# Rows transposed inside a projection's last group, three tiles begun on each half, and decode held and repaid there

## The chip, the cores and the metric

The kernel runs on one core of one Trainium2 chip. The metric is the device time of one execution in microseconds (us); the time of a kernel is the median of its runs. The core has a matrix engine (TensorE, PE in the profile, with its weight loads shown as PEld), a vector engine (VectorE, DVE), a scalar engine (ScalarE, ACT), a general engine (GpSimd, POOL), which here also issues the gathers of the decode part, and SyncE (SP), whose queue issues most weight loads. Each engine works through its own instructions in the order in which they were written into its queue, and waits where an instruction's data or buffer is not ready.

## The reference

One step of a decoder layer on two groups that share the weights: a prompt of 1024 rows of width 1024, and 8 sample rows, each with 8192 cached positions. For the prompt, `x` passes three blocks, each added to it:

```
xp = xp + merge_heads(fox_prompt(q, k, v, logf), sgu_prompt(u, z, ...), ..., w_o)   # attention + gating, out-projection w_o
xp = xp + cross_attend(rmsnorm(xp, g_cross), mk, mv, w_cq, w_co)                    # 256 memory tokens, 4 heads
xp = xp + conv_ffn(rmsnorm(xp, g_ffn), 0, w_up, conv_w, conv_b, w_down)             # MLP with a width-3 convolution
y  = rmsnorm(xp, g_final)
```

The sample rows go through the same layer, with attention over the cached keys and values (`cache_k`, `cache_v`, found through a page table). All matrices are fp32, and the prompt's products are made to nearly fp32 accuracy.

## The kernel before, in words

**Products.** A prompt product of fp32 operands is made of three matmuls of a faster type: each operand is split into a high part (ACT copies it, L235 or L238) and a low part (DVE subtracts, L236 or L239), and high x high, high x low and low x high are added up in one PSUM bank (`gemm3`, L272 to L274; in `out_proj` the same three stand at L1055 to L1057 and L1073 to L1075). With 8 slices of the contracted width a tile of 128 x 512 takes 24 matmuls. PSUM banks come from two pools: `BA` (tag `ba`, four banks) and `BB` (tag `bb`, two); `MM`, `TR` and `BK` are one function that takes from them in turn.

**Order of the prompt.** The 1024 rows are done in two halves of 512 rows (four row tiles of 128), one after the other: output projection `out_proj` with `w_o` (the stage is called `mid`), cross attention `cross` with its own `out_proj` with `w_co`, then the MLP `ffn`. Between an `out_proj` and the product after it stand the row norm and a transposition, because the next product needs the rows' columns on the partitions. That happens four times: into `cross` and into `ffn`, for each half. I call these places seams.

**At a seam.** `out_proj` makes its second 512 columns in the groups of row tiles (0), (1) and (2, 3). After each group `residual` (L1007, DVE) adds the result to the rows, and ACT sums their squares (L230). In front of `ffn` the rows are also scaled by their norm (`factor` on ACT and POOL, L1023 and L1024; `scaled` and `both` on ACT, L1036 and L1037); in front of `cross` they are not, since the norm is applied to the scores later. Then `norm_T` takes tiles 0 and 1: per pair of slices four transposes (L1106) into one bank and two splits out of it, each on ACT and DVE; then it calls `first`, which makes one tile of the next product on the first 256 rows. Then the same for tiles 2 and 3, and the other 256 rows of that one tile. All other tiles of the next product are made on 512 rows at once.

**Decode beside the prompt.** The sample rows are a second stream. `decode` makes 128 steps: each gathers a chunk of keys (L1407, POOL), multiplies it by the query on DVE (L1423) and reduces it there (L1427); value chunks are gathered at L1469 and multiplied on TensorE (L1475). `sample_rest` does the rest of the layer for the sample rows. The prompt's code yields its expected time `t` at many places; the loop at the end adds `t` to `acc[0]` and runs one step of the second stream for each `PACE` of it. While `held[0]` is set no step is taken, but the time still adds up, and is paid afterwards, at most one step or so at a yield. `held[0]` is set after group (2, 3) and cleared at the end of `norm_T`. What stands in each engine's queue in the end, and where, is decided by a planner that puts the instructions in order.

Of the kernel before, what the change touches and what calls it, by code (L numbers as in the profile page):

```python
# [30 lines left out]
NF = FF // P  # L31
# [47 lines left out]
def build(nc, tc, ctx, a, phases=None):  # L79
# [935 lines left out]
    def out_proj(w, mh, ml, xt, fetch=None, ys=None):  # L1015
# [26 lines left out]
        for n in range(2):  # L1042
# [24 lines left out]
            for group in ((0,), (1,), (2, 3)):  # L1067
                pss = [MM() for _ in group]
                for k in korder:
                    wh, wl = (ws[k // 2][q][:, k % 2, :] for q in range(2))  # L1070
                    for i, ps in zip(group, pss):
                        tb = slice(i * P, (i + 1) * P)
                        mmul(ps, mh[k][:, tb], wh, start=(k == korder[0]), stop=False)  # L1073
                        mmul(ps, mh[k][:, tb], wl, start=False, stop=False)
                        mmul(ps, ml[k][:, tb], wh, start=False, stop=(k == korder[-1]))  # L1075
# [14 lines left out]
    def norm_T(ys, g0, first):  # L1090


        hs, ls = [], []
        for t0 in (0, 2):
# [3 lines left out]
            for kk in range(0, 8, 2):  # L1098
                if t0 == 0:
                    h2, l2 = U([P, 2, 512], F32R), U([P, 2, 512], F32R)  # L1100
                    hs += [h2[:, 0, :], h2[:, 1, :]]
                    ls += [l2[:, 0, :], l2[:, 1, :]]
                tr = TR()
# [16 lines left out]
    def cross(xt, sq):  # L1120
# [12 lines left out]
        ws = [wload(wpair(a["w_cq"], kk, 0, 512), 1024) for kk in range(4)]  # L1133
        q2, ps0 = [], MM()
# [8 lines left out]
        hs, ls = yield from norm_T(xt, G_CROSS, lambda hs, ls, c: products(ps0[:, c], ws, 0, hs, ls, c))  # L1143
# [61 lines left out]
        for n in range(2):  # L1205
            if n:
                ws = [wload(wpair(a["w_cq"], kk, n * 512, 512), 1024) for kk in range(4)]
            for dt_ in range(4):
                if dt_ % 2 == 0:
                    q2.append(U([P, 2, 512]))  # L1210
                if n or dt_:
                    ps = MM()
                    products(ps, ws, dt_, hs, ls, slice(0, 512))
                else:
                    ps = ps0
# [29 lines left out]
        sq = yield from out_proj(a["w_co"], oh, ol, xt, ys=ys)  # L1245
        return ys
# [4 lines left out]
    def ffn(hf, xt, ys, late=None):  # L1251
        w0, pv0 = wload(a["w_up"][0], 1024), BK()

# [4 lines left out]
        hs, ls = yield from norm_T(ys, G_FFN, lambda hs, ls, c: up(pv0[:, c], w0, hs, ls, c))  # L1258
# [11 lines left out]
        for gi, gn in enumerate(GROUPS):  # L1270
            gh, gl = [], []
            for f in range(f0, f0 + gn):
                hc2 = []
                for part in range(2):
# [3 lines left out]
                    if ft:  # L1278
                        w_, pv = wload(a["w_up"][ft], 1024), BK()
                        up(pv, w_, hs, ls, slice(0, 512))  # L1280
                    else:
                        pv = pv0
# [548 lines left out]
    def prompt():  # L1831
# [38 lines left out]
        for hf in range(2):  # L1870
# [10 lines left out]
            sq = yield from out_proj(a["w_o"], mh, ml, xt, partial(load_x, hf))  # L1881
            if hf == 0:
                ys = yield from mix(cross(xt, sq), gating(1), 0.05)
            else:
                ys = yield from cross(xt, sq)
            phase[0] = f"ffn{hf}"
            sq = yield from ffn(hf, xt, ys, (lambda: ahead.append(merge(*merge_in(1))) or ahead[0]) if hf == 0 else None)
# [11 lines left out]
    seen = 0  # L1899
    for t in prompt():  # L1900
# [8 lines left out]
        acc[0] += t  # L1909
# [102 lines left out]
```

## Time and profile before

| | us |
|---|---|
| median of 3 runs | 1816.22 (1815.31 to 1817.39) |
| the profiled execution | 1820.56, its span 1818.4 |
| TensorE busy | 1745.0 (96%) |
| VectorE busy | 1397.5 (77%) |
| ScalarE busy | 734.4 (40%) |
| mean granted TensorE clock | 0.986 |

How to read it: the profile shows one execution. A row of a group names the line, the engine, the operation, the tile written and the tiles read, the count, the busy time and the mean of one, and then the idle time in front of it with what ended it. "PE bb L273 <- DVE u L239" says that TensorE's instruction of L273 waited for DVE's of L239. In a row of a stretch stand its start and end, its length, the busy time of the five engines with the count of instructions, the granted clock, the share of the DMA engines and GB/s. TensorE's matmuls overlap in the records, so the time of one is read from the distance of two starts. The first half's seams lie near 547 us (into `cross`) and 707 us (into `ffn`), the second half's near 1183 and 1351 us; the MLPs lie behind 722 and behind 1365 us.

### The profile page before, as it was taken

The numbers are of one execution on the slowest core, as the hardware profiler recorded it, in microseconds if no ns is written. First come the engines' busy times: TensorE is split into PE (matmuls) and PEld (weight loads), VectorE is DVE, ScalarE is ACT, GpSimd is POOL, SyncE is SP. The second block draws the span as 40 slices with busy tenths as digits, with TensorE's granted clock in tenths as the row PEclk, the third lists the DMA queues.
The fourth block names the chain that finished last, engine by engine and source line by source line (L and its number), as shares of the span: only waits on it lengthen the run. The fifth ranks groups of instructions, "written<-read, shape, count | busy, mean of one in ns | idle before, by whom it ended". The sixth has DMA issues, their size and how long they took to land.

```text
span 1818.4 us, 25090 instructions
## 1 busy us (share of the span) xinstructions
PE 1745.0 (96%) x9637; PEld 1294.9 (71%) x9637; DVE 1397.5 (77%) x1729; ACT 734.4 (40%) x1378; POOL 510.0 (28%) x461
## 2 busy tenths in 40 slices
PE   8999999888998999999999999989899999999997
PEld 5887776656676767777777776766576778767775
DVE  4689668888788877999989899898875549845344
ACT  6332365455643544433333244235353324332332
POOL 1252334332133432223332333334222111011110
PEclk9999999899999999999999999989999999999999
DMA  8886889777696986679878779988787777568982
GB/s 295 306 297 231 302 297 329 242 266 224 219 398 257 342 310 260 257 285 340 316 279 311 271 306 340 381 300 324 290 309 290 267 268 265 179 266 289 359 314 82
DMA packets 157074, 521.06 MB, mean 287 GB/s; under 512 B 20874, under 2 KB 40842, under 8 KB 124186
## 3 DMA queue, kind: packets, MB, share of 16 engines
q0 software_dynamic: 57168, 341.14, 49.5%
q1 hardware_dynamic: 92874, 165.73, 26.4%
q10 hardware_dynamic: 6912, 12.59, 1.8%
q8 instruction: 76, 1.25, 0.3%
q14 instruction: 44, 0.36, 0.1%
HBM read 495.47 MB, written 23.93 MB: 286 GB/s over the span
## 4 chain that ended last, share of the span: by engine, by line
PE 72%; DMA 10%; issue 7%; DVE 6%; ACT 2%; POOL 2%; SPq 0%; POOLq 0%; DVEq 0%; ACTq 0%
PE ba L272 11%; PE ba L274 11%; PE ba L273 11%; PE bb L272 5%; PE bb L273 5%; PE bb L274 5%; PE dv L1475 5%; DMA kv<-cache_k,io 3%; DMA wr<-w_in 2%; DMA kv<-cache_v,io 1%; PE dv L321 1%; PE dv L1751 1%; PE ba L1056 1%; PE ba L1055 1%; PE ba L1057 1%
## 5 line engine op out<-in xcount | busy, mean ns | idle before, releaser
L235 ACT ACTIVATE wh<-wr 128x1024 fp32r<-128x1024 f32 (+2 forms) x220 | 228.9, 1044 | 489.2 <-PE ba L273 156.0
L236 DVE TENSOR_TENSOR wl<-wr,wh 128x1024 fp32r<-128x1024 f32 (+2 forms) x220 | 262.5, 1200 | 175.6 <-PE ba L274 65.7
L1407 POOL DMA_INDIRECT kv<-cache_k,io x128 | 205.6, 1606 | 551.2 <-DVE s L1427 318.9
L1423 DVE TENSOR_TENSOR kv<-kv,d 128x1024 f32<-128x1024 f32 (+1 forms) x156 | 258.0, 1681 | 35.1 <-DMA kv<-cache_k,io 35.1
L1427 DVE TENSOR_REDUCE s<-kv 128x16 f32<-128x1024 f32 (+1 forms) x156 | 258.2, 1674 | 0.1
L1469 POOL DMA_INDIRECT kv<-cache_v,io x128 | 165.3, 1291 | 282.8 <-PE dv L1475 191.8
L272 PE MATMUL ba<-u,wh 128*128 128x512 f32 (+1 forms) x560 | 220.3, 395 | 1.7 <-ACT u L238 1.7
L273 PE MATMUL ba<-u,wh 128*128 128x512 f32 (+1 forms) x560 | 220.2, 393 | 1.7 <-DVE u L239 1.5
L274 PE MATMUL ba<-u,wl 128*128 128x512 f32 (+1 forms) x560 | 219.5, 393 | 0.0
L272 PE MATMUL ba<-wh,u 128*128 128x512 f32 (+1 forms) x495 | 186.9, 379 | 0.9 <-ACT u L235 0.9
L273 PE MATMUL ba<-wl,u 128*128 128x512 f32 (+1 forms) x495 | 185.4, 375 | 1.2 <-DVE wl L236 1.2
L274 PE MATMUL ba<-wh,u 128*128 128x512 f32 (+1 forms) x495 | 183.8, 376 | 0.0
L272 PEld LDWEIGHTS ba<-u,wh 128*128 128x128 f32 x560 | 106.8, 191 | 30.6 <-issue 5.6
L273 PE MATMUL bb<-u,wh 128*128 128x512 f32 (+1 forms) x304 | 119.4, 393 | 9.2 <-DVE u L239 9.2
L274 PEld LDWEIGHTS ba<-u,wl 128*128 128x128 f32 x560 | 106.9, 191 | 29.1 <-issue 6.1
L273 PEld LDWEIGHTS ba<-u,wh 128*128 128x128 f32 x560 | 106.7, 191 | 27.5 <-issue 2.7
L1475 PE MATMUL dv<-kv,s 128*32 128x512 f32 x1024 | 124.2, 598 | 1.8 <-DMA kv<-cache_v,io 1.8
L272 PE MATMUL bb<-u,wh 128*128 128x512 f32 (+1 forms) x304 | 119.4, 393 | 0.0
L274 PE MATMUL bb<-u,wl 128*128 128x512 f32 (+1 forms) x304 | 118.6, 390 | 0.0
L272 PEld LDWEIGHTS ba<-wh,u 128*128 128x128 f32 x495 | 93.0, 188 | 26.0 <-issue 6.9
L274 PEld LDWEIGHTS ba<-wh,u 128*128 128x128 f32 x495 | 92.8, 188 | 21.5 <-issue 3.7
L273 PEld LDWEIGHTS ba<-wl,u 128*128 128x128 f32 x495 | 93.1, 188 | 19.7 <-DVE wl L236 1.9
(425 smaller groups left out, 3255.9 us busy)
## 6 DMA issues: line engine op xcount, KB each, us to landing
wr<-w_up SPq DMA_DIRECT2D x88, 512.0 KB
kv<-w_up POOLq DMA_DIRECT2D x22, 1024.0 KB, 8.0
wr<-w_down SPq DMA_DIRECT2D x40, 512.0 KB
kv<-w_down POOLq DMA_DIRECT2D x11, 1024.0 KB, 8.5
wr<-w_in SPq DMA_DIRECT2D x16, 512.0 KB
wr<-w_o SPq DMA_DIRECT2D x16, 512.0 KB
wr<-w_cq SPq DMA_DIRECT2D x16, 512.0 KB
wr<-w_co SPq DMA_DIRECT2D x16, 512.0 KB
```

Source lines behind the costliest of these rows:

```text
L235: nc.scalar.activation(h, src, AF.Copy)
L236: nc.vector.tensor_tensor(l, src, h.bitcast(F32), op=ALU.subtract)
L272: mmul(out, sh, mh, start=(i == 0), stop=False)
L273: mmul(out, sh, ml, start=False, stop=False)
L274: mmul(out, sl, mh, start=False, stop=(i == n - 1))
L321: mmul(ps[32 * j : 32 * j + 32, :w], xT[:, k, :] if nk == 8 else xT[:, k * 8 : k * 8 + 32], raw[:, q, j * w : (j + 1) * w], start=(k == 0) ...
L1055: mmul(pss[i], mh[k][:, tb], wh, start=(k == korder[0]), stop=False)
L1407: nc.gpsimd.indirect_dma_start(kv, None, a["cache_k"], off(kidx[:, b, ch : ch + 1]))
L1423: nc.vector.tensor_tensor(kvv[:, i : i + m, :], kvv[:, i : i + m, :], qb.unsqueeze(1).broadcast_to((P, m, 512)), op=ALU.mult)
L1427: nc.vector.tensor_reduce(s[:, ch * 4 + i : ch * 4 + i + m, :].rearrange("p k h -> p (k h)"), kvv[:, i : i + m, :].rearrange("p k (h d) -> ...
L1469: nc.gpsimd.indirect_dma_start(kv, None, a["cache_v"], off(kidx[:, b, ch : ch + 1]))
L1475: mmul(dv[32 * j : 32 * j + 32, :], s[:, ch * 4 : ch * 4 + 4, :].rearrange("p k h -> p (k h)"), kvv[:, j, :], start=(ch == 1), stop=(ch == ...
```

## The change

- `out_proj` takes `hooks`. In the last group it calls, after each slice, the hooks listed for that slice: loads of the next product's first weights (after slices 1, 3, 5, 7, or 1, 3, 5 in front of `ffn`) and the four steps that transpose tiles 0 and 1. The last group takes its two banks from `BB`. The scaling of tile 1 moves from before that group's residuals to after its second slice.
- `norm_T` no longer runs through; it returns a generator `turn(t0)` for each pair of row tiles. The first pair's transposes go to `BA`, the second's to `BB`.
- `halves` begins three tiles of the next product, in three `BA` banks, on the first 256 rows; then it makes the transposes of tiles 2 and 3, and then the other 256 rows of the three tiles. It yields 2.8 for each of the six, and clears `held[0]` behind them.
- `cross` takes its first three query tiles from there, `ffn` the tiles 0, 22 and 1 of the up-projection.
- `held[0]` is set from the start of group (2, 3). The loop at the end no longer adds held time to `acc[0]`; it gathers it in `late`, and each later yield of `t` adds `t` and up to a quarter of `t` more out of `late`.

The number of transposes, splits, loads and decode steps stays the same; on TensorE 192 matmuls on 512 rows become 384 on 256 rows.

```diff
-    def out_proj(w, mh, ml, xt, fetch=None, ys=None):
+    def out_proj(w, mh, ml, xt, hooks, fetch=None, ys=None):
...
             for group in ((0,), (1,), (2, 3)):
-                pss = [MM() for _ in group]
-                for k in korder:
+                held[0] = len(group) == 2
+                pss = [BB() if held[0] else MM() for _ in group]
+                for at, k in enumerate(korder):
...
-                    if len(group) == 2 and k == korder[3]:
-                        yield 5.2
-                if ys is not None and group[0]:
-                    ys.append(scaled(group[0] - 1, factor(group[0] - 1)))
+                    if len(group) == 2:
+                        if ys is not None and at == 1:
+                            ys.append(scaled(1, factor(1)))
+                        for hook in hooks.get(at, ()):
+                            hook()
+                        if at == 3:
+                            yield 5.2
+                if ys is not None and group[0] == 1:
+                    ys.append(scaled(0, factor(0)))
                 for i, ps in zip(group, pss):
                     residual(xt, sq, i, n, ps)
-
-                held[0] = len(group) == 2
                 yield 5.2
...
-    def norm_T(ys, g0, first):
+    def norm_T(ys, g0):
...
-        for t0 in (0, 2):
+        def turn(t0):
...
-                tr = TR()
+                tr = BB() if t0 else BA()
...
-            first(hs, ls, c)
-            if t0 == 0:
-                yield 3
+        return hs, ls, turn
+
+    def ahead_of(turn, loads, at):
+
+        steps = turn(0)
+        hooks = {k: [partial(next, steps)] for k in at}
+        ws = []
+        for n, load in enumerate(loads):
+            hooks.setdefault(1 + 2 * n, []).insert(0, lambda load=load: ws.append(load()))
+        return hooks, ws
+
+    def halves(products, turn):
+
+        banks_ = [BA() for _ in range(3)]
+        for c in (slice(0, 256), slice(256, 512)):
+            if c.start:
+                for t in turn(2):
+                    yield t
+            for d, ps in enumerate(banks_):
+                products(ps[:, c], d, c)
+                yield 2.8
         held[0] = False
-        return hs, ls
+        return banks_
...
-        hs, ls = yield from norm_T(xt, G_CROSS, lambda hs, ls, c: products(ps0[:, c], ws, 0, hs, ls, c))
+        begun = yield from halves(lambda out, d, c: products(out, ws, d, hs, ls, c), turn)
...
+        hs, ls, turn = norm_T(ys, G_FFN)
+        hooks, ws = ahead_of(turn, [partial(wload, a["w_up"][ft], 1024) for ft in (0, NF, 1)], (3, 4, 5, 6))
+        yield from out_proj(a["w_co"], oh, ol, xt, hooks, ys=ys)
...
-        hs, ls = yield from norm_T(ys, G_FFN, lambda hs, ls, c: up(pv0[:, c], w0, hs, ls, c))
+        begun = yield from halves(lambda out, d, c: up(out, ws[d], hs, ls, c), turn)
+        begun = dict(zip((0, NF, 1), begun))
...
+            hs, ls, turn = norm_T(xt, G_CROSS)
+            hooks, ws = ahead_of(turn, [partial(lambda kk: wload(wpair(a["w_cq"], kk, 0, 512), 1024), kk) for kk in range(4)], (2, 3, 5, 6))
+            sq = yield from out_proj(a["w_o"], mh, ml, xt, hooks, partial(load_x, hf))
...
-        acc[0] += t
+        if held[0]:
+            late += t
+        else:
+            more = min(late, t / 4)
+            late -= more
+            acc[0] += t + more
```

More of the change, by code (lines that the diff above doesn't have):

```diff
@@ L1131, in cross @@
         fetch(1)
-        ws = [wload(wpair(a["w_cq"], kk, 0, 512), 1024) for kk in range(4)]
-        q2, ps0 = [], MM()
+        q2 = []
         def products(out, ws, dt_, hs, ls, c):
@@ L1210, in cross @@
                     q2.append(U([P, 2, 512]))
-                if n or dt_:
+                if n or dt_ > 2:
                     ps = MM()
@@ L1214, in cross @@
                 else:
-                    ps = ps0
+                    ps = begun[dt_]
                 nc.scalar.activation(q2[-1][:, dt_ % 2, :], ps[:, :512], AF.Copy)
@@ L1898, in build @@
     bgs.append(sample())
-    seen = 0
+    seen, late = 0, 0.0
     for t in prompt():
```

26 lines of the change are left out of this document (10 added, 16 removed).

## The prediction

> **What bounds the kernel now.** I read the page first, then the busy time by stretches, the waits of TensorE in the stretches that stood out, and the order in time there.
>
> ```profile
> span 1818.4 us, 25090 instructions
> PE 1745.0 (96%) x9637; PEld 1294.9 (71%) x9637; DVE 1397.5 (77%) x1729; ACT 734.4 (40%) x1378; POOL 510.0 (28%) x461
> ...
> PE 72%; DMA 10%; issue 7%; DVE 6%; ACT 2%; POOL 2%; SPq 0%; POOLq 0%; DVEq 0%; ACTq 0%
> ...
> L1407 POOL DMA_INDIRECT kv<-cache_k,io x128 | 205.6, 1606 | 551.2 <-DVE s L1427 318.9
> ```
>
> TensorE is the bound: busy 1745.0 of 1818.4 us, so a change that leaves its matmuls alone can win at most the 73 us of idle time, and what a lower granted clock costs. The change touches the four places where a projection ends and the next begins, which I call seams. Their rows (us, busy time of PE, PEld, DVE, ACT, POOL, then the granted clock), and then the rows of the stretches between them:
>
> ```profile
> 545.00:570.00 25.00, 21.82 (x128) 17.63 (x127) 24.20 (x38) 10.44 (x23) 6.89 (x6) 0.86 0.84 317
> 705.00:722.00 17.00, 13.89 (x74) 11.55 (x74) 12.50 (x26) 12.40 (x32) 4.78 (x6) 0.80 0.96 394
> 1182.00:1202.00 20.00, 13.96 (x89) 11.18 (x91) 18.36 (x30) 9.39 (x21) 6.82 (x5) 0.74 0.77 275
> 1350.00:1365.00 15.00, 13.38 (x84) 11.83 (x83) 10.79 (x22) 11.83 (x29) 1.10 (x2) 0.89 0.49 190
> ```
>
> ```profile
> 570.00:705.00 135.00, 131.54 (x643) 92.86 (x642) 109.02 (x129) 60.25 (x132) 52.22 (x32) 1.00 0.77 286
> 722.00:1182.00 460.00, 457.27 (x2165) 342.00 (x2165) 425.49 (x405) 163.64 (x257) 142.49 (x96) 1.00 0.81 305
> 1202.00:1350.00 148.00, 140.71 (x682) 96.91 (x683) 123.13 (x131) 59.82 (x131) 52.14 (x41) 0.99 0.86 319
> 1365.00:1785.00 420.00, 419.08 (x2793) 310.47 (x2795) 240.23 (x350) 137.98 (x237) 67.90 (x94) 1.00 0.75 274
> ```
>
> Idle at the seams: 3.18 + 3.11 + 6.04 + 1.62 = 13.95 us. The clock took (1 - clock) x busy = 0.14 x 21.82 + 0.20 x 13.89 + 0.26 x 13.96 + 0.11 x 13.38 = 10.9 us. So 24.9 us is all that the seams hold. Between them TensorE idles 3.46 + 2.73 + 7.29 + 0.92 = 14.4 us. TensorE's waits at the four seams, one answer each:
>
> ```profile
> PE bb L273 <- DVE u L239: 3.2, 3, 2.1
> ...
> PE ba L273 <- DVE u L239: 1.5, 1, 1.5
> PE ba L1106 <- ACT u L1036: 1.1, 1, 1.1
> ...
> PE bb L273 <- DVE u L239: 6.0, 2, 5.6
> ...
> PE ba L272 <- ACT u L238: 1.2, 2, 1.0
> ```
>
> So what ends last is the split of the transposed rows, its low part (L239) above all. At the third seam DVE is late because decode stands in its queue between the splits:
>
> ```profile
> 1189.27 0.86 DVE L239 SCALAR_TENSOR_TENSOR u<-ba,gp,u 128x256 fp32r<-128x256 f32 x2
> 1190.05 1.21 DVE L1427 TENSOR_REDUCE s<-kv 128x16 f32<-128x1024 f32 x1
> 1191.18 2.35 DVE L1423 TENSOR_TENSOR kv<-kv,d 128x1024 f32<-128x1024 f32 x2
> 1193.44 0.47 DVE L239 SCALAR_TENSOR_TENSOR u<-ba,gp,u 128x256 fp32r<-128x256 f32 x1
> ```
>
> **The change part by part.** *First-half transposes inside the last group.* The 16 transposes of tiles 0 and 1 and their 8 + 8 splits stay the same in number; they move under the last group's 48 matmuls. The rows that price this, from the order in time at the first seam and from the groups by form:
>
> ```profile
> 538.15 0.39 PE L1074 MATMUL ba<-wl,u 128*128 128x512 f32 x1
> ...
> 540.91 0.39 PE L1074 MATMUL ba<-wl,u 128*128 128x512 f32 x1
> ...
> 547.59 1.03 PE L1106 MATMUL ba<-cp,u 128*128 128x128 f32 x8
> 548.46 0.60 PE L1106 MATMUL bb<-cp,u 128*128 128x128 f32 x4
> ...
> 552.13 0.28 PE L272 MATMUL bb<-u,wh 128*128 128x256 f32 x1
> ...
> 552.84 0.28 PE L272 MATMUL bb<-u,wh 128*128 128x256 f32 x1
> ...
> 560.14 0.39 PE L273 MATMUL bb<-u,wh 128*128 128x256 f32 x1 [2.05 <-DVE u L239]
> ```
>
> ```profile
> L236 DVE TENSOR_TENSOR wl<-wr,wh 128x1024 fp32r<-128x1024 f32 x208 | 252.3, 1219 | 154.5 <-PE ba L274 65.7 <-issue 25.1 <-PE bb L274 16.4
> L1423 DVE TENSOR_TENSOR kv<-kv,d 128x2048 f32<-128x2048 f32 x68 | 154.4, 2280 | 11.7 <-DMA kv<-cache_k,io 11.7
> ...
> L1427 DVE TENSOR_REDUCE s<-kv 128x16 f32<-128x1024 f32 x88 | 104.1, 1211 | 0.0
> ...
> L1007 DVE TENSOR_TENSOR u<-ba,u 128x512 f32<-128x512 f32 x33 | 22.4, 687 | 15.1 <-PE ba L1075 9.4 <-PE ba L274 5.0 <-PE ba L1057 0.6
> ...
> L239 DVE SCALAR_TENSOR_TENSOR u<-ba,gp,u 128x256 fp32r<-128x256 f32 x44 | 19.6, 476 | 5.1 <-ACT u L238 5.1
> ```
>
> Twelve full matmuls start in 2.76 us, 0.230 each; the group lasts 48 x 0.230 + 16 transposes x 0.109 (0.87 / 8) = 12.8 us. In the order in which the changed kernel's instructions stand, DVE has in that time at the third seam 8 low splits (8 x 0.476), 3 weight splits (3 x 1.219) and one decode step (two halves to multiply and two to reduce, 4 x 1.21): 3.8 + 3.7 + 4.8 = 12.3 us. It fits, with 0.5 us to spare, so the cover is thin. If it is gone, TensorE waits inside the group by the excess: a late half step is 1.2 us. At the first seam the first transposes stand four matmuls (0.92 us) behind the last matmul of tile 1, whose residual (0.69) they read: no cost, or up to 1.2 us behind a decode half. Switching between transposes and products sixteen times in all is priced by no row; I put 1 us for it (bounds 0 and 2).
>
> *Three tiles begun on each half.* Six half matmuls start in 0.71 us, 0.118 each, against 0.115 for half of a full one: 4 seams x 2 more tiles x 48 halves = 384 x 0.003 = 1.2 us lost. In return TensorE has 72 x 0.118 = 8.5 us of work while the residuals of tiles 2 and 3, their transposes and splits are made; before it had 24 halves, 2.8 us. The residual chain behind the group's end is 0.69 + 1.22 (a weight split stands between) + 0.69 = 2.6 us, less the 0.69 us by which tile 2 ends earlier. In the two MLP seams, the row factor and the scaled copy come behind it:
>
> ```profile
> 713.18 0.29 ACT L1023 ACTIVATE fac<-sqx,part 128x1 f32<-128x1 f32 x1
> 713.37 0.62 ACT L230 ACTIVATE junk<-u 128x512 bf16<-128x512 f32 x1
> ...
> 715.31 1.33 ACT L1037 ACTIVATE u<-u,fac 128x512 f32<-128x512 f32 x2
> ```
>
> ```profile
> 713.55 0.54 POOL L1024 TENSOR_TENSOR fac<-fac,mhalf 128x1 f32<-128x1 f32 x1 [3.12 <-ACT fac L1023]
> ```
>
> That is 2.6 + 0.62 + 0.29 + 0.54 + two scalings 2 x 1.33 = 6.7 us, inside 8.5. What is late next: the first splits of the second half, which nothing covers behind their transposes, 0.48 on DVE and about as much on ACT, some 1.0 us at each seam: 4.0 us. And one place is not covered: at the second seam the order puts the low splits of k = 1, 3, 5, 7 of the *first* half behind both residuals on DVE. The fifth half matmul needs the first of them: 2.6 - 0.69 + 0.48 = 2.4 us after the group's end, while four halves last 0.47: 1.9 us idle. At the other three seams such splits stand before the residuals, or are needed some twenty halves later, and cost nothing.
>
> *The clock.* The row at 560.14 shows a 2.05 us gap, and the first seam's clock of 0.86 follows from it. At the fourth seam no single gap was over 1.0 us, and the clock is 0.89 all the same; there, 16 transposes in a row had gone ahead, and this row is the last half of them:
>
> ```profile
> 1351.80 1.07 PE L1106 MATMUL ba<-cp,u 128*128 128x128 f32 x8
> ```
>
> For the 1.9 us gap I take one loss like the first seam's, 3.1 us, and 1.4 (about the fourth's) for the three others together; bounds 0 and 10.9.
> The Trainium skill ("TensorE: Matmul & The Clock Gate", Part 1) has the clock halve after an idle window of about 3.4 us; the 2.05 us gap at the first seam is shorter, so the trace does not bear that figure out for a single gap. The Trainium skill (the same title, Part 4) also says that transposes do not count as busy as matmuls do; the fourth seam's row agrees. By the first seam's row the sum is the one below; by these two rules it is that of rival (a).
>
> *Weights loaded from the group.* The first w_cq or w_up loads keep their places on SP's queue within a few rows (they stood right behind the last w_o load already), so no DMA comes earlier than its buffer allows: 0. At the second seam POOL has one cache_k fetch (1.6 us) in front of tile 1's factor; 38 matmuls (8.7 us) stand there before the transposes that read the scaled tile, whose chain is 0.69 + 0.62 + 0.29 + 1.6 + 0.54 + 1.33 = 5.1 us: 0, with 3.6 us of room.
>
> *Decode held, then repaid at a quarter.* Counted in the order of DVE, decode steps per stage go from 17, 41, 4 and 20 (first cross stage, first MLP, second output projection, second cross stage) to 17, 43, 4 and 18. Two more steps in the MLP are 2 x 2 x 2.28 (multiply, and a reduce of the same size) = 9.1 us of DVE, whose idle time in 722 to 1182 is 34.5 us: 0 to 3 us, I take 0. Two fewer in the second cross stage take 9.7 us of DVE work out of 1202 to 1350, where TensorE idles most: 0 to -3, I take 0. The decode part ends earlier than before, and between 1365 and 1785 TensorE idles 0.92 us with it: 0.
>
> The sum: 24.9 at the seams, of which stay 4.0 + 1.9 idle and 3.1 + 1.4 clock = 10.4; 1.0 and 1.2 are added. Gain 24.9 - 12.6 = 12.3 us. The profiled execution took 1820.56 us, 1808.3 then; the median of the runs stands 4.3 lower at 1816.22, so 1804.
>
> **The rivals.** (a) *The clock does not fall.* If it is a long run of transposes with waits behind it that brought the drops, as at the fourth seam, then spreading them in fours among matmuls removes the cause, and a 1.9 us gap alone is too short: the 4.5 us come back too, 1799; with the split latencies hidden as well (4.0), 1795. For: the fourth seam's row. Against: the first seam's 2.05 us gap.
> The rules of the Trainium skill named above would give this rival.
>
> (b) *The waits only move.* The first transposes wait inside the group for late residuals (DVE has 0.5 us to spare at the third seam), 3 us at each seam with the clock: 12 us back, 1816. Against: DVE's busy time in the group is as it was, and TensorE's queue holds other matmuls between the runs.
>
> (c) *Slower: decode steps late in front of other splits.* Decode's fetches shift against the prompt from the first seam on, and in the cross stage each head's split stands behind a decode step on DVE:
>
> ```profile
> PE bb L1170 <- DVE u L236: 4.2, 1, 4.2
> ```
>
> ```profile
> 1275.38 2.36 DVE L1423 TENSOR_TENSOR kv<-kv,d 128x1024 f32<-128x1024 f32 x2 [4.81 <-DMA kv<-cache_k,io]
> ```
>
> One late fetch there cost 4.2 us. There are eight such splits in the two cross stages, and the order puts a decode step before most of them in both kernels. From three new ones (12.6 us) the gain is gone; five make 1804 + 21 = 1825. Against: only one in eight was late before.
>
> **How the numbers follow.** Forecast (1800 to 1811) 0.45; (a) 0.20; (b) 0.13; (c) 0.17, half of it reaching no further than 1820; rest 0.05. The forecast's own range is 1799 to 1810. The range for all, 1791 to 1822, takes in (a) with a late fetch removed (1795 - 4) and most of (c). A difference under 0.2% (3.6 us) can't be told from none here. Faster 0.71, same 0.10, slower 0.19.
>
> **What would show it.** The transposes in runs of four among the group's matmuls with no wait before them above 1 us; four seams with 5 to 7 us idle in all; at the second, a gap of about 2 us before a low-split matmul; clock rows of 0.93 or more at the other seams; TensorE's busy time down by about 4 us (6.4 us of slow clock gone, 2.2 added). The forecast is wrong if the idle time between the seams rises above 20 us, or if matmuls of the last group wait for residuals.

## The result, and the profile after

The changed kernel takes 1825.16 us (median of 16 runs, 1818.37 to 1836.22), beside 1815.93 for the kernel before on the same chips: 1.0053 times as long (95% interval 1.0040 to 1.0066). I had forecast 1804. It is slower by 9 us, and by more than the 0.2% that can be told apart. The profiled execution took 1825.52 us, so it stands at the median; that of before took 1820.56, 4.6 above its own.

The page of the changed kernel: span, busy time by engine, and the chain that ended last.

```profile
span 1823.7 us, 25476 instructions
PE 1748.8 (96%) x9829; PEld 1301.7 (71%) x9829; DVE 1397.4 (77%) x1725; ACT 737.7 (40%) x1378; POOL 507.8 (28%) x461
...
PE 44%; issue 13%; DVE 11%; DMA 9%; POOL 3%; ACT 2%; POOLq 0%; DVEq 0%; SPq 0%; ACTq 0%
```

TensorE carried 72% of the chain before and carries 44% now; "issue" (time in which an engine waited for nothing that the profile shows) and DVE have taken its place. That share alone orders nothing: a kernel below, h2, has 49% and takes 1815.9. The same eight stretches as in the prediction, in the changed kernel (busy PE, PEld, DVE, ACT, POOL, granted clock, DMA share, GB/s):

```profile
545.00:570.00 25.00, 25.00 (x201) 22.73 (x201) 18.77 (x30) 9.43 (x20) 8.91 (x5) 1.00 0.81 316
705.00:722.00 17.00, 16.71 (x124) 16.31 (x125) 4.09 (x10) 6.50 (x14) 0.98 (x2) 0.90 0.37 152
1182.00:1202.00 20.00, 20.00 (x106) 16.78 (x105) 14.75 (x19) 8.01 (x15) 2.80 (x3) 1.00 0.59 212
1350.00:1365.00 15.00, 15.00 (x109) 11.71 (x107) 9.13 (x16) 9.33 (x20) 3.92 (x5) 1.00 1.00 404
570.00:705.00 135.00, 129.22 (x635) 89.79 (x634) 123.30 (x149) 66.10 (x150) 51.59 (x37) 1.00 0.86 320
722.00:1182.00 460.00, 443.40 (x2090) 327.38 (x2089) 422.23 (x397) 159.57 (x251) 145.17 (x98) 0.98 0.81 304
1202.00:1350.00 148.00, 144.26 (x757) 101.25 (x755) 129.15 (x146) 66.06 (x143) 54.36 (x41) 1.00 0.87 323
1365.00:1785.00 420.00, 414.05 (x2806) 307.06 (x2805) 240.86 (x359) 141.56 (x246) 67.28 (x93) 1.00 0.73 268
```

The seams did close: in their four rows 13.95 us of idle time became 0.29, and the clock's 10.9 us became 1.7 (0.10 x 16.71). The stretches are cut where the seams of the kernel before lie. In the changed kernel the last groups end at 549.0, 701.7, 1199.9 and 1357.7 us; from 12 us before to 21 us behind those, TensorE idles 0.00, 3.61, 0.00 and 0.07 us. The 3.61 is a gap of 3.5 us at the second seam, which counts above in the row 570 to 705:

```profile
689.70:722.70 33.00, 29.39 (x198) 25.21 (x197) 18.31 (x30) 17.70 (x38) 7.36 (x8) 0.95 0.62 232
```

But the four stretches between them, 14.4 us idle before, now idle 5.78 + 16.60 + 3.74 + 5.95 = 32.1 us, 28.6 without that gap, and the clock takes 0.02 x 443.4 = 8.9 us in the first MLP. So in the eight rows together idle time rose by 4.0 us and slow clock fell by 1.8; with the 2.2 us that I had added for switches and half-width matmuls this is 4.4 of the span's 5.3. What was won was lost again, in this execution mostly in one place. TensorE's waits in the first MLP, before and after (us in all, times, longest):

```profile
PE bb L935 <- DVE u L239: 1.2, 1, 1.2
PE bb L274 <- DVE u L236: 1.2, 1, 1.2
PE ba L935 <- ACT u L235: 0.3, 1, 0.3
```

```profile
PE dv L1497 <- DMA kv<-cache_v,io: 5.3, 3, 4.7
PE ms L1482 <- DVE dg L1475: 3.1, 1, 3.1
PE bb L935 <- DMA u<-an_d: 3.1, 2, 1.8
PE ba L272 <- DVE u L1341: 2.1, 2, 1.3
PE dv L1497 <- ACT s L1485: 1.2, 1, 1.2
PE ba L935 <- DVE u L1007: 1.1, 1, 1.1
PE bb L935 <- DVE u L239: 0.6, 1, 0.6
```

Three of the seven (lines 1482 and 1497, 9.6 us) are matmuls of the decode, which stands in TensorE's queue between the prompt's. The longest gap, in the order in time of POOL, DVE and TensorE in the changed kernel:

```profile
797.77 1.34 POOL L1491 DMA_INDIRECT kv<-cache_v,io  x1 [15.75 <-PE dv L1497]
799.41 0.94 POOL L1491 DMA_INDIRECT kv<-cache_v,io  x1 [0.31 <-issue]
800.65 0.94 POOL L1429 DMA_INDIRECT kv<-cache_k,io  x1 [0.30 <-DVE s L1449]
801.90 1.11 POOL L1429 DMA_INDIRECT kv<-cache_k,io  x1 [0.31 <-DVE lps L1486]
```

```profile
811.88 2.29 DVE L1445 TENSOR_TENSOR kv<-kv,d 128x2048 f32<-128x2048 f32 x1 [8.29 <-DMA kv<-cache_k,io]
```

```profile
809.41 3.64 PE L1497 MATMUL dv<-kv,s 128*32 128x512 f32 x16 [4.66 <-DMA kv<-cache_v,io]
```

POOL waited 15.75 us for a gather buffer (there are four), which only a decode matmul far back in TensorE's queue frees. Then four gathers go out within 5 us, and both DVE and TensorE stand at the decode instructions that need them: 8.29 and 4.66 us, with the prompt's work behind them in both queues. The granted clock was 0.75 from 810 to 820. I read that as a decode that stands further ahead of its gathers than before. How long such a wait gets also differs from execution to execution: e4 below has the same order on DVE up to 846 us, and the same wait takes 2.79 us there:

```profile
811.18 1.06 PE L1497 MATMUL dv<-kv,s 128*32 128x512 f32 x8 [2.79 <-DMA kv<-cache_v,io]
```

### The profile page after: what moved, and what is told of

Same layout as the page of the kernel before. It is cut to its first block, busy times and chain, and to the rows that moved or that the text cites. A ratio compares the mean times of both kernels' runs of the same rounds, so it can differ in the third digit from the quotient of the medians.

```text
span 1823.7 us, 25476 instructions
## 1 busy us (share of the span) xinstructions
PE 1748.8 (96%) x9829; PEld 1301.7 (71%) x9829; DVE 1397.4 (77%) x1725; ACT 737.7 (40%) x1378; POOL 507.8 (28%) x461
## 4 chain that ended last, share of the span: by engine, by line
PE 44%; issue 13%; DVE 11%; DMA 9%; POOL 3%; ACT 2%; POOLq 0%; DVEq 0%; SPq 0%; ACTq 0%
PE ba L272 5%; PE ba L273 5%; PE ba L274 5%; PE dv L1497 4%; DMA kv<-cache_k,io 3%; DMA kv<-cache_v,io 2%; DMA kv<-w_up 2%; DVE wl L236 2%; PE bb L274 2%; PE bb L273 2%; PE bb L272 2%; DVE s L1449 2%; DVE kv L1445 1%; DMA u<-an_d 1%; PE ba L1056 1%
## 5 line engine op out<-in xcount | busy, mean ns | idle before, releaser
L236 DVE TENSOR_TENSOR wl<-wr,wh 128x1024 fp32r<-128x1024 f32 (+2 forms) x220 | 262.1, 1198 | 146.1 <-PE ba L274 48.6
L1429 POOL DMA_INDIRECT kv<-cache_k,io x128 | 194.0, 1516 | 544.6 <-DVE s L1449 335.0
L273 PE MATMUL ba<-u,wh 128*128 128x512 f32 (+1 forms) x656 | 237.6, 366 | 0.0
L274 PE MATMUL ba<-u,wl 128*128 128x512 f32 (+1 forms) x656 | 236.2, 363 | 0.0
L272 PE MATMUL ba<-u,wh 128*128 128x512 f32 (+1 forms) x656 | 231.9, 364 | 3.7 <-DVE u L239 3.5
L272 PE MATMUL ba<-wh,u 128*128 128x512 f32 (+1 forms) x521 | 199.1, 384 | 5.1 <-DVE u L1341 2.1
L273 PE MATMUL ba<-wl,u 128*128 128x512 f32 (+1 forms) x521 | 197.4, 380 | 1.3 <-DVE wl L236 1.3
L274 PE MATMUL ba<-wh,u 128*128 128x512 f32 (+1 forms) x521 | 194.5, 379 | 0.9 <-DVE u L236 0.9
L273 PEld LDWEIGHTS ba<-u,wh 128*128 128x128 f32 x656 | 124.0, 189 | 31.1 <-issue 10.3
L272 PEld LDWEIGHTS ba<-u,wh 128*128 128x128 f32 x656 | 121.5, 189 | 29.4 <-issue 5.6
L274 PEld LDWEIGHTS ba<-u,wl 128*128 128x128 f32 x656 | 123.9, 189 | 23.7 <-issue 4.0
L272 PEld LDWEIGHTS ba<-wh,u 128*128 128x128 f32 x521 | 99.3, 191 | 31.2 <-issue 6.3
L274 PEld LDWEIGHTS ba<-wh,u 128*128 128x128 f32 x521 | 98.7, 190 | 21.7 <-issue 1.2
L274 PE MATMUL bb<-u,wl 128*128 128x512 f32 x272 | 108.2, 398 | 0.0
L272 PE MATMUL bb<-u,wh 128*128 128x512 f32 x272 | 107.8, 396 | 0.0
L273 PE MATMUL bb<-u,wh 128*128 128x512 f32 x272 | 107.5, 396 | 0.0
```

The lines of the kernel that those rows point to most:

```text
L236: nc.vector.tensor_tensor(l, src, h.bitcast(F32), op=ALU.subtract)
L272: mmul(out, sh, mh, start=(i == 0), stop=False)
L273: mmul(out, sh, ml, start=False, stop=False)
L274: mmul(out, sl, mh, start=False, stop=(i == n - 1))
L1429: nc.gpsimd.indirect_dma_start(kv, None, a["cache_k"], off(kidx[:, b, ch : ch + 1]))
```

## The experiments

The decode's pace is set by an account (`acc`): each yield of the prompt pays in, each decode step costs the stage's `PACE`. I had costed the account's new rule at nothing, and had not added up what a seam pays in. Before, a seam pays 8 x 0.6 + 3 for the transposes and the first tile's half, and 3 x 5.2 when the three tiles are taken up: 23.4. After, it pays 4 x 0.6 + 6 x 2.8 in `halves`, and the same 3 x 5.2 again: 34.8. So there are three edits of the decode: the earlier hold, the quarter, and 11.4 more paid in a seam. The kernels below vary them; four more stand in the text alone. Every ratio is to the kernel before, on the same chip; from one set of runs to the next its median went from 1815.4 to 1818.1, so in a pair from two sets a difference under 3 us tells nothing.

| run | seams | hold from | payment | a begun tile brings | us | ratio (95%) |
|---|---|---|---|---|---|---|
| changed kernel | new | group's start | quarter | 5.2 | 1825.2 | 1.0053 (1.0040 to 1.0066) |
| e1_old_pay | new | start | at once | 5.2 | 1826.1 | 1.0060 (1.0041 to 1.0079) |
| j2_half_extra | new | start | at once | 3.3 | 1818.9 | 1.0008 (0.9990 to 1.0025) |
| i2_after_paid_as_before | new | start | at once | 1.4 | 1803.5 | 0.9930 (0.9909 to 0.9950) |
| j1_quarter_paid_as_before | new | start | quarter | 1.4 | 1825.2 | 1.0039 (1.0027 to 1.0051) |
| h1_after_paid_once | new | start | quarter | 0 | 1830.7 | 1.0085 (1.0065 to 1.0106) |
| e2_late_hold_old_pay | new | end | at once | 5.2 | 1818.4 | 1.0009 (0.9993 to 1.0025) |
| h2_paid_as_before | new | end | at once | 1.4 | 1815.9 | 1.0003 (0.9989 to 1.0017) |
| g2_paid_once | new | end | at once | 0 | 1806.8 | 0.9954 (0.9937 to 0.9970) |
| i3_late_hold_new_pay | new | end | quarter | 5.2 | 1823.8 | 1.0043 (1.0027 to 1.0059) |
| i4_paid_once_new_pay | new | end | quarter | 0 | 1813.9 | 0.9980 (0.9968 to 0.9992) |
| e3_before_new_pay | old | end | quarter | as before | 1821.6 | 1.0030 (1.0018 to 1.0042) |
| i1_before_early_hold | old | start | at once | as before | 1815.6 | 0.9997 (0.9977 to 1.0016) |
| h3_before_paid_more | old | end | at once | +11.4 a seam | 1811.4 | 0.9971 (0.9959 to 0.9984) |
| h4_before_paid_less | old | end | at once | -4.2 a seam | 1824.0 | 1.0041 (1.0025 to 1.0057) |

**First: payment, hold, or cover.** The edits, in this order: the payment undone; payment and hold undone; the payment alone on the kernel before; a higher price of a step.

```diff
 e1_old_pay (from the changed kernel), and the second edit of e2_late_hold_old_pay
-        if held[0]:
-            late += t
-        else:
-            more = min(late, t / 4)
-            late -= more
-            acc[0] += t + more
+        acc[0] += t
 e2_late_hold_old_pay: the hold set after the group
-                held[0] = len(group) == 2
-                pss = [BB() if held[0] else MM() for _ in group]
+                pss = [BB() if len(group) == 2 else MM() for _ in group]
...
+                held[0] = len(group) == 2
                 yield 5.2
 e3_before_new_pay: the first edit backwards, on the kernel before
 e4_pace95 (from the changed kernel)
-PACE = {... 'ffn0': 8.5, ...}
+PACE = {... 'ffn0': 9.5, ...}
```

> The changed kernel with the old payment: the time of every yield goes straight onto the decode's account, held or not, and nothing is repaid at a quarter. Theory 'payment' (the quarter's repayment puts decode steps ahead of their gathers in the first MLP, where TensorE's idle time rose from 2.7 to 16.6 us): the idle time there falls back below 6 us and the time to 1812-1816. Theory 'hold' (the hold begins 11 us earlier, the gathers stop with it: DMA was idle for 12 us in the seam ahead of the first MLP) and theory 'cover' (the seam is now filled with TensorE's work alone, so that DVE falls behind there and TensorE waits later): no change, 1822-1828, with 14-18 us of idle time in the first MLP.

> The changed kernel without both edits of the decode: it is held only after the last group, as before, and paid as before; the transposes inside the last group and the three begun tiles stay. Theory 'hold': the gathers go on through the last group, TensorE's idle time in the first MLP falls from 16.6 to below 6 us, the seams stay filled to within 4 us in all, and the time is 1806-1812, faster than before. Theory 'cover': 1820-1828, the idle time in the MLP stays above 12 us. If DVE's decode work delays the transposes' splits in the last group, the seams lose 2-5 us each instead, 1815-1822.

> The kernel before with the new payment alone (held time kept apart and repaid at a quarter; it is held where it was held before). One decode step of 66 stands later at the fourth tile of the first MLP, and no count differs by more than one. Theory 'payment': slower by 4-10 us. Theories 'hold' and 'cover': within 2 us of the kernel before. If the place of single steps matters by itself, the idle time between the seams, 14.4 us, moves by more than 3 us either way.

> The changed kernel with the first MLP's price of a decode step at 9.5 in place of 8.5: nothing differs up to its 24th tile of 44, and from there three steps fewer are done by the end of the stage (100 in place of 103; the kernel before has 101). Theory 'payment', in the form that too many steps are put into the first MLP: idle time after the 24th tile falls by 5 us or more, the time to 1818-1821. Theories 'hold' and 'cover', which put the loss into the stage's first half: 1824-1828, and the idle time before the 24th tile is unchanged.

Measured: 1826.1, 1818.4, 1821.6, and 1824.0 for the last (1.0056, 1.0037 to 1.0075). Undoing the payment alone does not bring the changed kernel back (e1), though adding it costs 6 us on the kernel before (e3). e4 empties the first MLP, and it does not help: the row idles 4.03 us in place of 16.60, and the last group of the third seam ends at 1182.6 in place of 1199.9 us. But a wait of 5.0 us comes up at the fourth seam (the transposes of L1110 behind a low split of weights, L236), and from the end of the last group there the rest takes 483.7 us in place of 466.0:

```profile
722.00:1182.00 460.00, 455.97 (x2185) 342.10 (x2184) 421.53 (x408) 167.38 (x266) 134.54 (x94) 1.00 0.80 301
```

So the idle time of the first MLP alone is not what the time follows: work of the decode that is not done there is done later (behind the fourth seam's last group POOL starts 20 gathers in e4 and 12 in the changed kernel). e2 beside e1 seemed to say that the hold costs 8 us; the last experiments show that it does not.

**Second: is the decode's work on DVE what can't keep up, and what do the tiles and the account do.** The light kernels leave three quarters of the decode's multiply and reduce out.

```diff
 f1_before_light (from the kernel before), f2_after_light (from the changed kernel)
-    kvv[:, i : i + m, :], kvv[:, i : i + m, :], qb.unsqueeze(1).broadcast_to((P, m, 512))
+    kvv[:, i : i + m, :128], kvv[:, i : i + m, :128], qb[:, :128].unsqueeze(1).broadcast_to((P, m, 128))
...
-    kvv[:, i : i + m, :].rearrange("p k (h d) -> p (k h) d", d=64)
+    kvv[:, i : i + m, :128].rearrange("p k (h d) -> p k h d", d=16)
 g1_one_tile (from e2_late_hold_old_pay)
-            for d, ps in enumerate(banks_):
-                products(ps[:, c], d, c)
-                yield 2.8
+            products(banks_[0][:, c], 0, c)
+            yield 2.8
+        for d in (1, 2):
+            products(banks_[d][:, :512], d, slice(0, 512))
+            yield 5.2
 g2_paid_once (from e2_late_hold_old_pay; the same at the query tiles of cross)
-                    yield 5.2
+                    yield 5.2 if new else 0.0
```

> The kernel before with the decode's multiply and reduce cut to 16 of 64 elements of each head wherever it runs in wide steps (work left out: the scores are wrong; gathers, waits, TensorE's share and the order's logic are as before). This is the base for the next run. The four seams keep their idle time where it hangs on the prompt's own splits: 8-14 us; between them 5-14 us; time 1800-1814.

> The changed kernel with the same cut. Theory 'cover' (the time won in the seams is given back because the decode, on DVE and in its gathers, can't keep up with the faster prompt): with the decode light on DVE the gain of the seams stays, 8-14 us faster than the light kernel before. If instead the decode's gathers alone set it (four buffers, 1 MB each), the changed kernel is within 4 us of the light kernel before, or slower, with TensorE's waits for cache_v still there. If the loss has nothing to do with the decode, it is 5-10 us slower, as with the whole decode.

> The changed kernel with the decode held and paid as before, and one tile of three begun in halves; the second and third follow whole, behind the second half's transposes. If the three begun tiles carry the filling of the seams: the second half's splits show again, 1-4 us of idle time in each of the two seams ahead of the MLPs, and the time is 1820-1826 beside 1818.4 with three. If the transposes inside the last group do it alone: 1816-1820. Theory 'cover': idle time that comes back in the seams goes from the stages between them, 1816-1820.

> The changed kernel with the decode held and paid as before, and begun tiles paid once: the time of a tile begun in halves (2 x 2.8) is no longer paid again when the tile is taken up (5.2). Two steps fewer are done by the twelfth tile of the first MLP (68 in place of 70 in the kernel before and 72 with the double pay). Theory 'payment', in the form that the prompt runs ahead of the time that it is credited with: idle time in the first MLP falls from 9.7 to 3-6 us and the time to 1808-1814, faster than before. Theory 'cover': less decode in the seams, no gain, 1817-1823.

Measured: 1793.1 and 1813.7 for the light pair, 1823.0 with one tile (1.0044, 1.0028 to 1.0060), 1806.8 with begun tiles paid once. "Cover" falls: with 335 us less work on DVE (1397.5 to 1062.7 in the two kernels of before) the changed kernel is 20 us slower than its base, not faster. The first MLP has no idle time at all there (460.00 of 460.00 us busy); the light kernel loses elsewhere, most of all on a load in the cross stages (4.3 us in the first and 9.1 us in the second, `t` from `o_mk` at L1175). This wait is in no profile of the changed kernel or its variants with the whole decode, so the light pair says only that DVE's amount of work is not the cause. One tile instead of three costs 4.6 us against e2, and their intervals just miss each other. g2 is the first that beats the kernel before; it differs from e2 in the credit alone.

**Third: the credit.**

```diff
 h1_after_paid_once: g2's edit in the changed kernel
 h2_paid_as_before: g2 with 1.4 in place of 0.0
 h3_before_paid_more (from the kernel before)
-                yield 3
+                yield 14.4
 h4_before_paid_less (from the kernel before)
-                yield 0.6
+                yield 0.45
...
-                yield 3
+                yield 0.0
```

> The changed kernel whole, with its early hold and its quarter repayment, and begun tiles paid once (as in g2). Three to four steps fewer stand ahead of the twelfth tile of the first MLP (66 in place of 69). Theory 'payment' (begun tiles paid twice put the decode ahead of its gathers; that alone costs the changed kernel its gain): 1805-1813, faster than the kernel before. If the early hold costs by itself, as e1 beside e2 suggests (1826 and 1818): 1812-1818.

> The changed kernel with the decode held and paid as before, and a seam credited with the same sum as in the kernel before: a tile that is taken up brings 1.4 in place of 5.2 (in g2: 0). The steps at the tiles of the first MLP are then within one of the kernel before. Theory 'payment': the seams' gain stays, 1806-1812. If only less credit than before brings the gain (g2 has 4.2 less a seam): 1814-1818, like the kernel before.

> The kernel before with 11.4 more credited in each of its four seams, which is what the changed kernel pays beyond it; nothing else differs. Two steps more stand ahead of the twelfth tile of the first MLP. Theory 'payment': slower by 4-10 us, with TensorE waiting for the decode's cache_v or for splits between the seams. Theory 'cover': within 3 us of the kernel before.

> The kernel before with 4.2 less credited in each seam, which is what g2 pays less than it. A control for g2: if less credit helps any order, 1807-1812, and g2's 1806.8 is not the seams' gain. If the seams carry g2's gain, this one stays within 3 us of the kernel before, 1813-1819.

Measured: 1830.7, 1815.9, 1811.4, 1824.0. None of the four came as the theory that more credit costs had it; h2 came in its second range, by which only less credit than before brings a gain. It is also the plainest test of the seams: its hold, its payment and its sum per seam are those of the kernel before, and it is level with it. On the kernel before, more credit makes it faster by 5 us and less makes it slower by 8: where the steps fall matters there more than how many there are. h1 fails in its own way, at the very end, where the decode's last weights come late:

```profile
PE dv L321 <- DMA kv<-w_down: 9.2, 7, 3.6
```

**Fourth: hold, payment and credit apart.**

```diff
 i1_before_early_hold (from the kernel before)
             for group in ((0,), (1,), (2, 3)):
+                held[0] = len(group) == 2
                 pss = [MM() for _ in group]
...
-                held[0] = len(group) == 2
                 yield 5.2
 i2_after_paid_as_before: e1 with 1.4 for a begun tile; j2_half_extra: e1 with 3.3
 i3_late_hold_new_pay: e2 with the quarter back; i4_paid_once_new_pay: i3 with 0.0 for a begun tile
 j1_quarter_paid_as_before: the changed kernel with 1.4 for a begun tile
```

> The kernel before with the hold alone moved: the decode is held from the start of the last group instead of its end, and paid as before. No transpose moves. If the early hold costs by itself (e1 beside e2: 1826 and 1818; the gathers stand still for longer): 1820-1826, while the seams lose no more than before (13.9 us of idle time). If the place of single steps is what moves the time, in either direction: anything between 1810 and 1824, and the seams may even gain, since DVE is freer.

> h2 (1815.9) with the changed kernel's early hold: the transposes and three tiles as changed, the decode held from the start of the last group, the account credited in a seam with the same sum as in the kernel before, and no quarter. If the early hold costs by itself: 1821-1827. If not: 1812-1819.

> The changed kernel with the hold alone put back behind the last group; the quarter repayment stays. It completes the square with the changed kernel (early, quarter: 1825.2), e1 (early, at once: 1826.1) and e2 (late, at once: 1818.4). If the hold costs and the payment doesn't: 1815-1821. If the payment costs too, as on the kernel before (e3: +6): 1821-1826.

> The neighbour of the fastest kernel so far (g2, 1806.8): the same, with the held time repaid at a quarter; one step fewer at some tiles. If g2's gain is that of its seams, this one is at 1803-1812. If g2 owes it to where single steps happen to stand: 1812-1824, or a longer tail, as in h1, which paid late too.

> The changed kernel whole, with one thing undone: a tile that is taken up brings 1.4 in place of 5.2, so that a seam credits the same sum as in the kernel before. The quarter repayment stays. If the double credit is what cost the changed kernel its gain: 1804-1814. The quarter cost 5 to 7 us in three of four pairs (e3, i3, i4), so 1808-1812 if both act as they did. If the quarter with the early hold leaves the decode late at the end, as in h1: a longer tail and 1815-1828.

> i2 (1803.5) and e1 (1826.1) differ in the credit of a tile that is taken up alone: 1.4 and 5.2. This is 3.3, half way. At the twelfth tile of the first MLP 69 steps stand, as in e1; in i2 it is 68, at the sixteenth 76 and 74. If the number of steps ahead in the first MLP is the cause: near e1, 1818-1826. If the time follows the credit evenly: 1812-1818. Outside 1803-1826: the place of single steps scatters it.

Measured: 1815.6, 1803.5, 1823.8, 1813.9, 1825.2, 1818.9. i2 came below both ranges that I had written for it. Read in pairs that differ in one edit:

- *The early hold*: e1 beside e2 +7.7 us, the changed kernel beside i3 +1.4, i1 beside the kernel before -1.3, i2 beside h2 -12.4. Both signs: the hold is not the cause. Nor is the pause that it puts into the gathers: in i2, the fastest, the DMA engines were busy 0.23 of the time at the second seam, less than the 0.37 of the changed kernel.
- *The quarter*: e3 +6, i3 beside e2 +5.3, i4 beside g2 +7.1, j1 beside i2 +21.7, the changed kernel beside e1 -1.0. It costs in four pairs of five.
- *The double credit*: with the early hold and payment at once, 5.2, 3.3 and 1.4 for a begun tile give 1826.1, 1818.9 and 1803.5. With the late hold 5.2, 1.4 and 0 give 1818.4, 1815.9 and 1806.8. With the quarter it is -9.9 (i4 beside i3), 0 (j1 beside the changed kernel) and +5.5 (h1, with its late end).

In the first row of credits the waits for gathers fall with the credit, 535 to 1350 us on DVE and 535 to 1380 us on TensorE: e1, then j2, then i2.

```profile
DVE kv L1445 <- DMA kv<-cache_k,io: 30.2, 12, 7.3
...
PE dv L1497 <- DMA kv<-cache_v,io: 8.1, 5, 3.6
```

```profile
DVE kv L1446 <- DMA kv<-cache_k,io: 23.4, 17, 4.5
...
PE dv L1498 <- DMA kv<-cache_v,io: 2.1, 1, 2.1
```

```profile
DVE kv L1446 <- DMA kv<-cache_k,io: 22.6, 12, 5.9
...
PE dv L1498 <- DMA kv<-cache_v,io: 1.0, 1, 1.0
```

In the changed kernel these are 34.4 and 6.9 us, and DVE's fall in the second row as well (28.7, 20.9, 18.3). They do not order all kernels, though: e4 has 20.6 on DVE and takes 1824, the kernel before has 28.5 and takes 1816. Late gathers are thus one way in which a badly placed step costs, not the only one. With the quarter it is another: j1 waits for cache_v no longer than j2 does (1.7 us in the first MLP), and loses its time to the prompt's own splits. Its longest waits in the first MLP and at the fourth seam:

```profile
PE ba L272 <- ACT u L235: 6.2, 3, 3.6
...
PE ba L272 <- DVE u L239: 5.7, 1, 5.7
```

Which decode step stands in front of which split there was not settled. j1 idles more than i2 in three places above all: 12.49 against 6.01 us in the first MLP, 5.97 against 0.24 at the fourth seam (it lies near 1339 us in j1, near 1332 in i2), and 9.62 against 5.59 behind it. j1, then i2, with i2's second seam first:

```profile
722.00:1182.00 460.00, 447.51 (x2111) 328.78 (x2111) 429.81 (x406) 159.76 (x254) 147.84 (x102) 0.99 0.84 312
1327.00:1360.00 33.00, 27.03 (x167) 22.81 (x166) 19.10 (x26) 16.82 (x31) 8.03 (x8) 0.90 0.67 253
1365.00:1785.00 420.00, 410.38 (x2755) 300.86 (x2754) 243.96 (x355) 142.05 (x240) 72.00 (x97) 1.00 0.76 280
```

```profile
705.00:722.00 17.00, 16.76 (x141) 15.83 (x143) 6.70 (x15) 8.21 (x18) 1.56 (x2) 1.00 0.23 86
722.00:1182.00 460.00, 453.99 (x2167) 337.62 (x2160) 435.69 (x415) 167.08 (x265) 154.13 (x102) 1.00 0.84 316
1320.00:1353.00 33.00, 32.76 (x243) 28.52 (x245) 19.47 (x32) 18.81 (x37) 6.04 (x7) 1.00 0.61 235
1365.00:1785.00 420.00, 414.41 (x2745) 305.80 (x2744) 235.63 (x349) 136.51 (x238) 65.22 (x92) 1.00 0.73 265
```

i2 keeps the transposes, the three tiles and the early hold of the change, drops the quarter, and pays a seam as before. It beats both kernels, and its 1803.5 us is what I had forecast for the whole change. It is not the rule, though: h2 differs from it in the hold alone and takes 1815.9.

## Why the prediction was wrong

**First-half transposes inside the last group: right.** They stand in short runs, mostly of four (one of nine at the second seam), with no wait before them, as the order in time at the first seam shows:

```profile
538.08 0.60 PE L1110 MATMUL ba<-cp,u 128*128 128x128 f32 x4
538.44 0.47 PE L1074 MATMUL bb<-wh,u 128*128 128x512 f32 x1
538.75 0.39 PE L1075 MATMUL bb<-wl,u 128*128 128x512 f32 x1
538.98 0.40 PE L1076 MATMUL bb<-wh,u 128*128 128x512 f32 x1
```

The switch costs nothing that shows, against 1 us taken: from the first transpose to the second matmul behind the four it is 538.75 - 538.08 = 0.67 us, which is what four transposes (4 x 0.109) and one matmul (0.23) take by themselves. Rival (b), waits inside the group, did not come: nothing waits at the first, third and fourth seam.

**Three tiles begun: right in the sum, wrong at one seam.** I had left 1.0 us at each seam for the first splits of the second half; the four seams hold 0.29 us in all by the rows, beside the gap at the second. For the second seam I had 1.9 us, as low splits stand behind both residuals on DVE; the profile has 3.5 there (TensorE's wait for L239), 3.6 in e1, but none in i2 with the same instructions of the prompt (0.2 us in all at that seam, for L238). The order of decode and splits on DVE sets it, not the residuals alone.

**The clock: better than forecast in the seams.** I had kept 4.5 us; three seams granted 1.00 and the second 0.90, which is 1.7 us. This is what rival (a) had for the clock, but its reason, the run of transposes, is not borne out (last section). I had read the fourth seam's 0.89 as the work of sixteen transposes; finer rows put it behind small gaps that add up to 1.4 us. The whole span gained none of it: the mean granted clock is 0.986 in both kernels. By length times (1 - clock), the seams (33 us each) went from 13.7 to 1.7 us, but the stretches between them from 1.7 to 8.5, and what lies ahead of the first, where the order on DVE is the same in both, from 8.5 to 11.9. TensorE's busy time, forecast to fall by 4 us, rose by 3.8.

**"Decode held, then repaid at a quarter ... I take 0": this is the step that failed**, and with it the assumption that the 14.4 us between the seams stay. I bounded the cost by the amount of DVE work (9.1 us more, in 34.5 us of idle time) and compared step counts by stage. The count was nearly unchanged and told nothing: as far as the runs show, what costs is where a step stands against its gather and against the prompt's splits in three queues that keep their order. Those 14.4 us became 32.1, or 28.6 without the gap at the second seam. Two parts of the step were missing: the extra 11.4 credited in each seam, which I did not see, and the quarter, which I priced by the steps that it moves. Either alone spoils the gain with the early hold (e1 1826.1 and j1 1825.2); without both, the rest of the change gives 1803.5. At the seams the sum was sound: of the 24.9 us there, some 5.5 are left (3.8 idle and 1.7 of clock), where I had left 10.4. The zero had no fixed price: with the early hold the two edits cost 22 us, but h2, with nothing of them and the late hold, is at 1815.9 and idles 19 us between its seams, so that undoing all three edits of the pacing wins back 9 us and none of the forecast gain. Where the single steps fall is worth that much by itself, and it is partly luck that i2 meets my 1804. What stays open is why: none of the counts or waits that I read sorts all of these kernels.

**Rival (c)** named late decode steps and the right time (1825, at 0.17), which is luck, since it had the wrong place and the wrong queue: the longest waits are of the decode's own matmuls on TensorE, not of the prompt's splits behind a step on DVE. For the place, I put it in the cross stages, which idle less than before from 1202 to 1350 (3.74 against 7.29 us). In the changed kernel it sat in the first MLP, where I saw 34.5 us of idle DVE and took it for room. The line that I had set for being wrong, more than 20 us idle between the seams, is the one that was crossed.

## What to carry to other kernels

Where one program interleaves two streams by a written order, an edit that speeds one stream also moves the other against it: add up what the change pays into the pacing, and treat its price as unknown in both directions, not as zero. Here the account alone moved the unchanged prompt by -5 to +8 us, and the changed one by 22, more than the 12 us that I had forecast for the change itself. Test such a change with its parts apart: with the seams as changed and the account as before, one place of the hold gave a kernel faster than both (i2), the other one that is level with the kernel before (h2). A stage that idles less can also only have passed its work on, as in e4, so judge by the time of the whole.

## What was not expected of the hardware

It needs no long gap to bring the granted clock down, and it goes down for 3.4 us at a time, to half. In i2 one gap of 2.60 us ends at 1540.1; in the kernel before, at the fourth seam, gaps of at most 1.04 us add up to 1.42 us from 1353.4 to 1356.8 (i2 first):

```profile
1537.30:1540.70 3.40, 0.80 (x4) 0.50 (x4) 3.40 (x5) 0.00 (x0) 0.73 (x1) 1.00 0.02 8
1540.70:1544.10 3.40, 3.13 (x8) 1.92 (x6) 3.40 (x5) 1.51 (x2) 0.00 (x0) 0.50 0.87 286
```

```profile
1350.00:1353.40 3.40, 3.20 (x25) 2.61 (x23) 3.12 (x5) 2.42 (x6) 0.12 (x1) 1.00 0.98 364
1353.40:1356.80 3.40, 1.98 (x11) 1.39 (x11) 2.91 (x7) 3.18 (x11) 0.99 (x2) 1.00 0.99 398
1356.80:1360.20 3.40, 3.40 (x18) 3.40 (x17) 1.23 (x4) 3.10 (x6) 0.00 (x0) 0.51 0.19 77
```

In the changed kernel waits of at most 1.9 us between 1550 and 1570 left it at 1.00, though one such stretch (1555.7 to 1559.1) held 1.74 us of idle time; so the sum that it takes is not fixed by these rows. The Trainium skill ("TensorE: Matmul & The Clock Gate", Part 1) has the clock halve after an idle window of about 3.4 us; these rows show a loss after less, and the measurement decides. What the Trainium skill says of transposes (the same title, Part 4), that they don't count as busy as matmuls do, is not borne out at the fourth seam: its first sixteen transposes lie between 1350.8 and 1352.9, and the stretch in front of the slow one holds none.
